# Second block of a one-core kernel: where the convolution's gate and norm, the last head steps, the key and query norms and the first expert products stand

## The chip, the cores and the metric

The kernel runs on one core of a Trainium2 chip. The metric is the device time of one execution in microseconds. The core has five engines that run their own instruction lists: PE (matrix products), ACT and DVE (element by element), POOL, and SP, which here issues nearly all loads. Engines wait for each other through semaphores.

## The reference

256 tokens of width 1024 pass two blocks. The first (a pooling mixer, an attention, two MLPs) is not touched. The second is, cut to what matters:

```python
hn = rms_norm_2(h, attn_norm_g)
xc, b_gate, c_gate, q, k, v = split(hn @ w_in)
y = b_gate * causal_depthwise_conv(c_gate * xc, conv_w)      # width 512, 3 taps
y_conv = rms_norm_2(y in groups of 64) * conv_out_g
q = rms_norm_2(q, per 64) * q_norm_g / 8 ; k = rms_norm_2(k, per 64) * k_norm_g
a = softmax(q0 k0^T) - lam * softmax(q1 k1^T)                # 4 heads of 128, causal
y_attn = rms_norm_2(a @ v, per head) * subln_g * (1 - lam_init)
h = h + concat(y_conv, y_attn) @ w_out
hn2 = rms_norm_2(h)
g = argmax(hn2 @ w_router_group)                             # 1 of 4 groups
top 2 of the 8 experts of that group, softmax of the two
h = h + sum over 32 experts: comb * ((silu(hn2 @ w_gate) * (hn2 @ w_up)) @ w_down)
```

## The kernel before

**Weights.** All weights are fp32 in DRAM. Class Weights streams them in order through a ring of 1 MB slots: `pump` issues a load on SP (L90) whenever the slot that was used longest ago is free. A dense weight is used in halves of 128x1024: `split` writes a high part on ACT (L107) and the rest on DVE (L108), the tile wp; when the second half of a slot is split, the slot is free. `take()` hands out the next half, `look(n)` splits n halves ahead, `W.ahead` is the number that `take` splits ahead by itself, `W.held` keeps slots from being used again. `open_ring`, `state_ring` and `parts_ring` turn memory that has become free into further slots. The 32 experts' weights are used whole, with no split; `W.done(NE)` frees four slots after half of a gate, up or down product. An expert's capacity is a tile of CAP tokens, and four experts (NE) make one pass p; eight passes (NP) do all 32.

**Order.** Every engine runs its instructions in the order in which the Python code issues them; nothing reorders them afterwards. Generators (`proj`, `proj_tok`, `normed`, `conv_out`) are advanced by `steps`, so that the code writes by hand which piece of a product or a norm comes next. PSUM has four single banks (tag A) and two pairs (tag B).

**Key and query norms.** `proj` makes q (pq) and k (pk), `proj_tok` makes v (pv). `normed` has three steps: squares (gq), then the mean by a product (gstat) with c2 added (kn, L909) and Ln and Exp on ACT (L911, L912), then `newton` (ku, L300 to L304) and the scaling that gives kn (L917). `x_tokens` turns the residual into tokens (product xkb, copy xk L1034); `x_stat_end` gives the mean of squares xstat, from which `rsq` makes r (ry on ACT L310 and L311, ru and r on DVE), and c2 is made from it (L1072). rt and tcol bring r and c2 into columns. The queries' sums of squares are the 16 small products qs, then qa and rq. The tiles gq, kn, ku, ry and ru share six buffers of the tag t2, taken in turn.

**Heads.** `h0(h)` makes the scores z, the maxima m (L934) and the softmax pr (ACT L940, DVE L944 to L948); `h1` transposes it (L955), `h2` multiplies with v and squares, `h3` takes the mean and Ln and Exp, `h4` ends the norm with `newton` and splits the result into mh and ml (L317, L318), the input of the last product wout.

**Convolution.** pc, px, pb are the three projections; `conv_u` and `conv_y` (yc, L995) make the taps, `conv_gate` multiplies by b_gate and squares, `conv_out(i)` takes the mean by a product, adds c2 (cn, L1015), Ln, Exp, `newton` and two splits into mh and ml. `out_piece(s)` is a quarter of half of the product with w_out; pieces 0 to 3 use the heads, 4 to 7 the convolution.

**Experts.** `h_add` adds the residual (xk), `h_transpose` and `logits` lead to the router on DVE; warm products keep PE at work; rank (five products), rk (L1310), the one-hot oh, `gather` (32 records of gb, then eight copies xg), `first_products` (gu), `hidden`, `down_products` (dn).

```python
    nk = normed(steps(pk, 4), kn, g2[:, 1:2])
    steps(nk)
    steps(pq, 2)
    x_tokens(0, 0)
    steps(pq)
    x_tokens(0, 1)
    p = x_stat_end(xs, "A")
    rsq(p, EPS, r, T)
    DVE.tensor_scalar(c2, p, EPS, EPS, op0=OP.add, op1=OP.mult)
```

## Time and profile before

| | |
|---|---|
| median of 3 runs | 1117.42 us (1117.38 to 1337.03) |
| profiled execution: its own time, its span | 1116.21 us, 1114.5 us |
| mean granted clock of PE | 0.969 of full |
| PE busy | 981.5 us, 88% of the span |
| DVE busy | 485.4 us, 44% |
| ACT busy | 389.6 us, 35% |
| loads | 306.58 MB, mean 275 GB/s over the span |

Busy shares are averages over stages with different limits. All times below are us from the start of the span of the profiled execution. [...] A matmul in the rows may count as two records where it makes two passes.

### The profile page before, as it was taken

What the parts mean: (1) busy time and instruction counts of PE and PEld (TensorE: products, weight loads), DVE (VectorE), ACT (ScalarE), POOL (GpSimd) and SP (SyncE); (2) the same over time, 40 slices, a digit from 0 to 9 for tenths busy, and PEclk for the clock granted to TensorE, in tenths of its full rate; (3) what the DMA queues carried; (4) which work ended last, traced back from release to release, by engine and by line L of the source; (5) the groups of instructions that cost most, each with busy time, mean ns of one, the idle gap of its engine ahead of it and who ended that gap; (6) DMA issues with size and microseconds to landing.
All of it is one profiled execution on the core that took longest, in us unless ns stands there. A gap on an engine that the chain in (4) does not pass through costs nothing.

```text
span 1114.5 us, 16629 instructions
## 1 busy us (share of the span) xinstructions
PE 981.5 (88%) x6999; PEld 729.9 (65%) x6999; DVE 485.4 (44%) x843; ACT 389.6 (35%) x602; POOL 11.4 (1%) x31
## 2 busy tenths in 40 slices
PE   9899999999999999999999989887777766777666
PEld 7899999998889999999979764232222221212212
DVE  8865554795448845655987763010101010100101
ACT  6554444563766534444566522000000000000000
POOL 3000000000000000000000000000000000000000
PEclk9999999999999999999999999999989999888997
DMA  8465565437222654555374787999999999999997
GB/s 310 146 226 186 199 195 188 151 115 256 84 77 81 242 200 159 168 211 189 107 309 152 264 330 313 421 420 421 420 422 421 420 422 421 421 421 420 421 412 260
DMA packets 79895, 306.58 MB, mean 275 GB/s; under 512 B 8033, under 2 KB 13770, under 8 KB 56266
## 3 DMA queue, kind: packets, MB, share of 16 engines
q1 hardware_dynamic: 79818, 305.49, 71.4%
q8 instruction: 56, 0.92, 0.3%
q14 instruction: 21, 0.17, 0.0%
HBM read 304.42 MB, written 1.05 MB: 274 GB/s over the span
## 4 chain that ended last, share of the span: by engine, by line
PE 51%; DMA 37%; DVE 8%; ACT 3%; issue 1%; SPq 0%; DVEq 0%; ACTq 0%
PE pj L156 20%; PE acc L156 17%; DMA w<-in_w_exp_up 12%; DMA w<-in_w_exp_gate 12%; DMA w<-in_w_exp_down 12%; PE z L156 3%; PE wo L156 2%; PE pv L156 2%; PE gu L156 1%; DVE xT L450 1%; DVE wp L108 1%; DVE xt L447 1%; PE wout L156 1%; DVE xl L453 1%; ACT wp L107 1%
## 5 line engine op out<-in xcount | busy, mean ns | idle before, releaser
L108 DVE TENSOR_TENSOR wp<-w,wp 128x1024 fp32r<-128x1024 f32 x194 | 230.4, 1223 | 86.1 <-ACT wp L107 86.0
L156 PE MATMUL gu<-w,xg 128*32 128x512 f32 x1024 | 186.7, 654 | 75.0 <-DMA w<-in_w_exp_up 43.6
L107 ACT ACTIVATE wp<-w 128x1024 fp32r<-128x1024 f32 x194 | 196.3, 1050 | 87.2 <-PE pj L156 41.8
L156 PE MATMUL acc<-uh,wp 128*128 128x256 f32 x1024 | 187.0, 283 | 0.0
L156 PEld LDWEIGHTS gu<-w,xg 128*32 128x32 f32 x1024 | 40.6, 118 | 206.0 <-DMA w<-in_w_exp_up 77.0
L156 PE MATMUL pj<-xh,wp 128*128 128x256 f32 x1216 | 173.0, 284 | 1.9 <-DVE ev L406 1.9
L156 PEld LDWEIGHTS acc<-uh,wp 128*128 128x128 f32 x1024 | 160.7, 192 | 0.1
L156 PEld LDWEIGHTS pj<-xh,wp 128*128 128x128 f32 x1216 | 157.2, 192 | 2.7 <-PE px L156 2.4
L156 PE MATMUL acc<-ul,wp 128*128 128x256 f32 x512 | 144.9, 283 | 0.0
L156 PE MATMUL dn<-w,sT 128*32 128x512 f32 (+1 forms) x544 | 82.1, 627 | 33.6 <-DMA w<-in_w_exp_down 23.9
L156 PE MATMUL pj<-xl,wp 128*128 128x256 f32 x608 | 98.4, 283 | 0.0
L156 PEld LDWEIGHTS acc<-ul,wp 128*128 128x128 f32 x512 | 98.3, 192 | 0.1
L156 PEld LDWEIGHTS pj<-xl,wp 128*128 128x128 f32 x608 | 84.1, 192 | 0.0
L318 DVE TENSOR_TENSOR yl<-dn,yh 128x512 fp32r<-128x512 f32 x15 | 10.4, 692 | 164.5 <-ACT yh L317 164.5
L156 PEld LDWEIGHTS dn<-w,sT 128*32 128x32 f32 x544 | 21.2, 118 | 88.0 <-DMA w<-in_w_exp_down 43.4
L317 ACT ACTIVATE yh<-dn 128x512 fp32r<-128x512 f32 x15 | 9.0, 597 | 197.0 <-PE dn L156 128.7
L1409 DVE SCALAR_TENSOR_TENSOR silu<-silu,cs,gu 128x512 f32<-128x512 f32 x8 | 8.9, 1108 | 133.3 <-PE gu L156 133.3
L1336 ACT ACTIVATE xg<-gb,ffn 128x128 f32<-128x128 f32 x32 | 9.2, 369 | 128.7 <-PE gb L156 128.7
L532 DVE TENSOR_TENSOR usq<-relu 128x512 f32<-128x512 f32 x32 | 22.0, 687 | 48.9 <-ACT relu L531 48.9
L156 PE MATMUL px<-xh,wp 128*128 128x256 f32 x224 | 33.2, 291 | 4.4 <-ACT wp L107 3.4
L531 ACT ACTIVATE relu<-pj 128x512 f32<-128x512 f32 x28 | 16.4, 587 | 56.4 <-PE pj L156 56.4
L156 PEld LDWEIGHTS gb<-oh,xk 128*128 128x128 f32 x256 | 29.2, 192 | 7.4 <-PE gu L156 4.2
(353 smaller groups left out, 1038.9 us busy)
## 6 DMA issues: line engine op xcount, KB each, us to landing
w<-in_w_exp_gate SPq DMA_DIRECT2D x64, 1024.0 KB, 19.9
w<-in_w_exp_up SPq DMA_DIRECT2D x64, 1024.0 KB, 19.8
w<-in_w_exp_down SPq DMA_DIRECT2D x60, 1024.0 KB, 19.8
w<-in_w_down SPq DMA_DIRECT2D x32, 1024.0 KB, 5.8
w<-in_w_up SPq DMA_DIRECT2D x28, 1024.0 KB, 7.1
w<-in_w_in SPq DMA_DIRECT2D x10, 1024.0 KB, 12.2
w<-in_w_kv SPq DMA_DIRECT2D x6, 1024.0 KB
w<-in_w_up SPq DMA_DIRECT2D x8, 512.0 KB
```

The lines of the kernel that those rows point to most:

```text
L107: self.nc.scalar.activation(h, raw, AF.Copy)
L108: self.nc.vector.tensor_tensor(lo, raw, h.bitcast(F32), OP.subtract)
L156: PE.matmul(o, l, r, start=start, stop=stop, skip_group_check=True)
L317: ACT.activation(h, src, AF.Copy)
L318: DVE.tensor_tensor(lo, src, h.bitcast(F32), OP.subtract)
L447: DVE.scalar_tensor_tensor(t, self.y[:, k] if k < 2 else self.banks[k // 2][:, (k % 2) * 256:(k % 2 + 1) * 256], self.gain(k), self.r, op0 ...
L450: DVE.tensor_tensor(xT[:, k], xT[:, k], t, OP.add)
L453: DVE.scalar_tensor_tensor(lo[l], xT[:, l], g(l), h[l].bitcast(F32), op0=OP.mult, op1=OP.subtract)
L531: ACT.activation(r, b[i], AF.Relu)
L532: DVE.tensor_tensor(u, r, r, OP.mult)
L1336: ACT.activation(dst, src, AF.Identity, scale=g)
L1409: DVE.scalar_tensor_tensor(sv, sv, CSL[p][1], of(u), op0=OP.mult, op1=OP.mult)
```

## The change

In the first part (before the first head) xstat, c2 and the Ln and Exp of r are issued ahead of the first `x_tokens`, the key norm's second step comes after the third step of pq, r's Newton step after it; the key norm's last step moves behind rt and tcol, and the qs products are issued in four groups of two between the matmuls of the first step of pv (`query_stat`); `W.look(5)` goes. In the second part (after `conv_y(1)`) the last projection pb yields after each of its four half pieces; `h4(2)`, `h3(3)`, `conv_gate`, `h4(3)` and the first step of `conv_out(0)` stand between them, `W.ahead` is set to 2 and then 0, single `look(3)` calls take the place of the `look(6)` calls, and the closing of the attention's memory, with the ring slots that it gives, comes after the whole of pb. In the third part the two warm matmuls behind rank write a bank of their own; `gather` stops after 12 of its 16 gb products and the first half of the first gate product comes ahead of the last four; xg is written by ACT and DVE in turn.

```diff
--- before.py
+++ after.py
@@ -476,7 +476,7 @@
         return p
-    def proj(xh, xl, tag="B", stagger=None, turned=False, post=None):
+    def proj(xh, xl, tag="B", stagger=False, turned=False, post=None):
         b = [post.px[:, i] for i in range(2)] if post else pair(tag, "pj")
@@ -500,10 +500,8 @@
             two = [W.take(), W.take()]
             for i in range(2):
                 for s in (2, 3):
-                    if s == 3:
-                        stagger(None, i)
                     piece(s, *two[s - 2], (2 * i, 2 * i + 1))
-                stagger(b[i], i)
+                    yield b
         if post:
             b = post.whole()
             W.ahead = was
@@ -696,7 +694,7 @@
                        channel_multiplier=-1)
     V = st.tile([128, 2, D], F32, name="V", tag="xtok")
-    def proj_tok(xh, xl, tag):
+    def proj_tok(xh, xl, tag, between=iter(())):
         b = pair(tag, "pv")
         for s in range(4):
@@ -708,6 +706,7 @@
                     for t in range(2):
                         mm(b[t], a[k][:, t * 128:(t + 1) * 128], w[:, c], start=k == 0 and w is h and a is xh,
                            stop=k == 7 and a is xl)
+                    next(between, None)
             yield None
         yield b
@@ -995,18 +994,9 @@
                 DVE.scalar_tensor_tensor(yc[:, k], src, w, yc[:, k], op0=OP.mult, op1=OP.add)
     def conv_gate(b, i):
-        if b is None:
-            if i == 0:
-                h3(3)
-                h4(2)
-                h4(3)
-        else:
-            v = flat(yc[:, 2 * i:2 * i + 2])
-            DVE.tensor_tensor(v, v, b, OP.mult)
-            cq.append(norm_square(v, 512))
-            if i == 0:
-                aq_stack.close()
-                open_ring("ring0", RINGS[1])
+        v = flat(yc[:, 2 * i:2 * i + 2])
+        DVE.tensor_tensor(v, v, b, OP.mult)
+        cq.append(norm_square(v, 512))
     def conv_out(i):
         b = bb[i]
@@ -1034,9 +1024,19 @@
         ACT.activation(dst, of(b), AF.Copy)
     pq, pk = proj(anh, anl, "B", turned=True), proj(anh, anl, post=P)
-    pv = proj_tok(anh, anl, "A")
+    def query_stat():
+        for t in range(2):
+            for j in range(4):
+                o = t * 8 + 2 * j
+                mm(qs[:, o:o + 2], sq[j // 2][:, (j % 2) * 256 + t * 128:(j % 2) * 256 + (t + 1) * 128], blk2, start=True,
+                   stop=True)
+                if j % 2:
+                    yield
+    pv = proj_tok(anh, anl, "A", query_stat())
     cq = []
-    pc, px, pb = proj(anh, anl, "A"), proj(anh, anl, "A"), proj(anh, anl, "A", conv_gate)
+    pc, px, pb = proj(anh, anl, "A"), proj(anh, anl, "A"), proj(anh, anl, "A", True)
     def steps(g, n=1):
         for _ in range(n):
@@ -1064,12 +1064,16 @@
     nk = normed(steps(pk, 4), kn, g2[:, 1:2])
     steps(nk)
     steps(pq, 2)
+    p = x_stat_end(xs, "A")
+    DVE.tensor_scalar(c2, p, EPS, EPS, op0=OP.add, op1=OP.mult)
+    y, ry = [tmp.tile([128, 512], F32, name="ry", tag="t2", bufs=6)[:, :T] for _ in range(2)]
+    ACT.activation(y, p, AF.Ln, bias=eps)
+    ACT.activation(y, y, AF.Exp, scale=-0.5)
     x_tokens(0, 0)
     steps(pq)
+    steps(nk)
+    newton([(p, EPS, y, ry, r)])
     x_tokens(0, 1)
-    p = x_stat_end(xs, "A")
-    rsq(p, EPS, r, T)
-    DVE.tensor_scalar(c2, p, EPS, EPS, op0=OP.add, op1=OP.mult)
     u = act.tile([128, 4 * (T + 2)], F32, name="u", tag="x3").rearrange("p (k t) -> p k t", t=T + 2)
     POOL.memset(u[:, :, 0:2], 0.0)
     steps(pq)
@@ -1078,7 +1082,6 @@
     x_tokens(1, 0)
     x_tokens(1, 1)
     state_ring("xT")
-    steps(nk)
     rt = bank("A", "rt")
     for i, a in enumerate((r, c2)):
@@ -1089,17 +1092,12 @@
     DVE.scalar_tensor_tensor(r, r, 0.25, r, op0=OP.mult, op1=OP.mult)
     rcol = aq.tile([128, 2], F32, name="rcol")
     DVE.tensor_scalar(rcol, tcol[:, 0:2], -0.5, None, op0=OP.mult)
+    steps(nk)
     qs = bank("A", "qs")
-    for t in range(2):
-        for j in range(4):
-            o = t * 8 + 2 * j
-            mm(qs[:, o:o + 2], sq[j // 2][:, (j % 2) * 256 + t * 128:(j % 2) * 256 + (t + 1) * 128], blk2, start=True,
-               stop=True)
+    steps(pv)
     qa = aq.tile([128, 2, 8], F32, name="qa")
     for t in range(2):
         DVE.tensor_scalar(qa[:, t], qs[:, t * 8:(t + 1) * 8], tcol[:, 2 + t:3 + t], None, op0=OP.add)
-    steps(nk)
     new_mix(mixh, 1, "mh", "uh")
     new_mix(mixl, 1, "ml", "ul")
     for i in range(2):
@@ -1107,8 +1105,7 @@
     rsq(flat(qa), 0.0, flat(rq), 16)
     DVE.tensor_scalar(rq, rq, -0.5, None, op0=OP.mult)
     gate_consts()
-    W.look(5)
-    steps(pv, 2)
+    steps(pv)
     h0(0)
     steps(pv)
     vb = steps(pv, 2)
@@ -1144,14 +1141,28 @@
     h1(3)
     h3(2)
     conv_y(1)
+    h4(2)
     steps(pb)
     h2(3)
     conv_y(2)
     new_mix(mixl, 0, "ml", "x3")
+    W.ahead = 2
+    steps(pb)
+    h3(3)
     bb = steps(pb)
+    conv_gate(bb[0], 0)
+    steps(pb)
+    h4(3)
+    co = [conv_out(0), conv_out(1)]
+    steps(co[0])
+    W.ahead = 0
+    W.look(3)
+    steps(pb)
+    conv_gate(bb[1], 1)
+    aq_stack.close()
+    open_ring("ring0", RINGS[1])
     state_ring("xh")
     state_ring("xl")
-    W.look(6)
     ob = [two_banks("wout") for _ in range(2)]
@@ -1164,17 +1175,18 @@
                     mm(ob[t][:, i], a[k][:, f], w[:, i * 512:(i + 1) * 512], start=s == 0 and w is h and a is mixh,
                        stop=s == 7 and a is mixl)
-    co = [conv_out(0), conv_out(1)]
     out_piece(0, *W.take())
     steps(co[0])
+    steps(co[1])
+    W.look(3)
     out_piece(1, *W.take())
+    W.look(3)
     steps(co[1])
+    out_piece(2, *W.take())
+    W.look(3)
     W.held = True
-    W.look(6)
-    steps(co[0])
-    out_piece(2, *W.take())
+    W.look(5)
     parts_ring()
-    steps(co[1])
     out_piece(3, *W.take())
     parts_ring()
@@ -1305,7 +1317,7 @@
             mm(o, onesb, sel[:, 0], stop=True)
     for t in range(2):
         mm(rkp[:, 64:96], onesb, sel[:, t], stop=t == 1)
-    warm(rkp[:, 128:384], xk[:, 0, 0:T], 2, ident)
+    warm(bank("A", "warm")[:, :T], xk[:, 0, 0:T], 2, ident)
     rk = small("rk", 2, 32)
     DVE.scalar_tensor_tensor(rk, rkp[:, 0:64].rearrange("p (t e) -> p t e", t=2), 1.0, sel, op0=OP.add, op1=OP.mult)
@@ -1321,22 +1333,41 @@
     def gather(p):
         XG[p] = hx.tile([128, KT, 128], F32, name="xg", tag="hx")
         for i in range(2):
             b = bank("A", "gb")
             for j in range(4):
+                if i and j == 2:
+                    yield
                 f = slice((4 * i + j) * 128, (4 * i + j + 1) * 128)
                 for t in range(2):
                     mm(b[:, j * 128:(j + 1) * 128], xk[:, t, f], OHT[p][t], start=t == 0 and j == 0, stop=t == 1)
             for j in range(4):
                 dst, src, g = XG[p][:, 4 * i + j], b[:, j * 128:(j + 1) * 128], ffn[:, 4 * i + j:4 * i + j + 1]
-                if i:
+                if j % 2:
                     DVE.tensor_scalar(dst, src, g, None, op0=OP.mult)
                 else:
                     ACT.activation(dst, src, AF.Identity, scale=g)
+        yield
+    def first_products(p, i, halves_=range(2), b=None):
+        b = bank("A", "gu") if b is None else b
+        for h in halves_:
+            n = 6 * NE * p + 2 * NE * i + NE * h
+            for kk in range(4):
+                k = 4 * h + kk
+                for j in range(NE):
+                    mm(b[j * CAP:(j + 1) * CAP], XG[p][:, k, j * CAP:(j + 1) * CAP],
+                       W.whole(n + j)[:, kk * 512:(kk + 1) * 512], start=k == 0, stop=k == 7)
+            W.done(NE)
+        return b
     onehot(0)
-    gather(0)
+    first_gather = gather(0)
+    next(first_gather)
+    first_gate = first_products(0, 0, (0,))
+    next(first_gather)
     ms, rr, u = sm[:, 0:2], sm[:, 4:6], sm[:, 6:8]
     DVE.tensor_tensor(ms, sm[:, 0:4:2], sm[:, 1:4:2], OP.add)
     DVE.tensor_scalar(ms, ms, 1.0 / D, EPS, op0=OP.mult, op1=OP.add)
@@ -1389,18 +1420,6 @@
                                  accum_out=c[:, NE + 1:NE + 2])
         DVE.tensor_copy(c[:, NE:NE + 1], b[:, 256 + NE:257 + NE])
         CSL[p] = ot, c[:, NE + 1:NE + 2], c[:, NE:NE + 1]
-    def first_products(p, i, halves_=range(2), b=None):
...
     def hidden(p, g, u):
         s = mo.tile([128, 512], F32, name="silu", tag="silu")
@@ -1452,7 +1471,7 @@
     for p in range(NP):
         if p:
             y = parts_of(YS[p - 1][0])
-        g = first_products(p, 0, (0,))
+        g = first_products(p, 0, (0,)) if p else first_gate
         if p:
             combine(p - 1, y, 0, 512)
             y = parts_of(YS[p - 1][1])
@@ -1465,7 +1484,8 @@
         u = first_products(p, 1)
         s = hidden(p, g, u)
         if p + 1 < NP:
-            gather(p + 1)
+            for _ in gather(p + 1):
+                pass
         sT = down_products(p, s)
         if p == 1:
```

How the lists of three engines change, with the waits as the compiled program has them.

ACT, from the wp copy after the squares of the keys; before (xk is the residual in tokens, ry and kn are Ln and Exp of r and of the key norm, gq squares):

```order
L107 ACTIVATE wp<-w 128x1024 [waits PE_49]
L1034 ACTIVATE xk<-xkb 128x128x4 [waits PE_49]
L107 ACTIVATE wp<-w 128x1024 [waits DMAHW1_49]
L1034 ACTIVATE xk<-xkb 128x128x4 [waits PE_49]
L310 ACTIVATE ry<-xstat,eps 128x256 [waits PE_49]
L311 ACTIVATE ry<-ry 128x256 [waits Activation_49]
L107 ACTIVATE wp<-w 128x1024
L895 ACTIVATE gq<-pj 128x512 [waits PE_49]
L895 ACTIVATE gq<-pj 128x512
L1034 ACTIVATE xk<-xkb 128x128x4 [waits PE_49] x2
L911 ACTIVATE kn<-kn 128x512 [waits DVE_49,Activation_49]
L912 ACTIVATE kn<-kn 128x512 [waits Activation_49]
```

and after:

```order
L107 ACTIVATE wp<-w 128x1024 [waits PE_49]
L1070 ACTIVATE ry<-xstat,eps 128x256 [waits DVE_49]
L1071 ACTIVATE ry<-ry 128x256 [waits Activation_49]
L1024 ACTIVATE xk<-xkb 128x128x4 [waits PE_49]
L107 ACTIVATE wp<-w 128x1024 [waits DMAHW1_49]
L910 ACTIVATE kn<-kn 128x512 [waits DVE_49]
L911 ACTIVATE kn<-kn 128x512 [waits Activation_49]
L910 ACTIVATE kn<-kn 128x512 [waits DVE_49]
L911 ACTIVATE kn<-kn 128x512 [waits Activation_49]
L1024 ACTIVATE xk<-xkb 128x128x4 [waits PE_49]
L107 ACTIVATE wp<-w 128x1024
L894 ACTIVATE gq<-pj 128x512 [waits DVE_49,PE_49]
```

The Ln of xstat (L310, now L1070) has moved ahead of the first xk copy and waits for DVE where it waited for PE; the keys' Ln and Exp (L911, now L910) now stand ahead of the last three xk copies, of a wp copy and of the queries' squares.

DVE at the same place; before (c_5881 is c2, ku the Newton step of the key norm):

```order
L1072 TENSOR_SCALAR c_5881<-xstat 128x256
L108 TENSOR_TENSOR wp<-w,wp 128x1024 [waits PE_49,Activation_49]
L909 TENSOR_TENSOR kn<-gstat,c_5881 128x512 [waits DVE_49,PE_49]
L909 TENSOR_TENSOR kn<-gstat,c_5881 128x512 [waits PE_49]
L1088 COPY tcol<-rt 128x4 [waits PE_49]
L1089 SCALAR_TENSOR_TENSOR r<-r 128x256
L1091 TENSOR_SCALAR rcol<-tcol 128x2 [waits DVE_49]
L1101 TENSOR_SCALAR qa<-qs,tcol 128x8 [waits PE_49]
L1101 TENSOR_SCALAR qa<-qs,tcol 128x8
L300 TENSOR_TENSOR ku<-kn 128x512 [waits Activation_49]
```

and after:

```order
L1068 TENSOR_SCALAR c_5881<-xstat 128x256 [waits PE_49]
L108 TENSOR_TENSOR wp<-w,wp 128x1024 [waits DMAHW1_49,Activation_49]
L908 TENSOR_TENSOR kn<-gstat,c_5881 128x512 [waits DVE_49,PE_49]
L908 TENSOR_TENSOR kn<-gstat,c_5881 128x512 [waits PE_49]
L300 TENSOR_TENSOR ry<-ry 128x256
L302 SCALAR_TENSOR_TENSOR ry<-xstat,ry 128x256 [waits DVE_49]
L304 SCALAR_TENSOR_TENSOR r<-ry 128x256 [waits DVE_49]
L108 TENSOR_TENSOR wp<-w,wp 128x1024 [waits Activation_49]
L1091 COPY tcol<-rt 128x4 [waits PE_49]
L1092 SCALAR_TENSOR_TENSOR r<-r 128x256 [waits DVE_49]
L1094 TENSOR_SCALAR rcol<-tcol 128x2 [waits DVE_49]
L300 TENSOR_TENSOR ku<-kn 128x512 [waits PE_49,Activation_49]
```

c2 has moved between wp subtractions, r's Newton step behind the key norm's kn; qa no longer stands ahead of ku, and the first ku waits for PE too (the third group of qs, which reads the buffer that ku takes).

PE at the end of the second block, from the last rank product; before:

```order
L156 MATMUL rank<-bf 128x32
L156 MATMUL rank<-xk,ident 128x256 x2
L156 MATMUL gb<-oh,xk 128x128 [waits DVE_49,PE_49]
L156 MATMUL gb<-oh,xk 128x128 [waits DVE_49]
L156 MATMUL gb<-oh,xk 128x128 x6
L156 MATMUL gb<-oh,xk 128x128 [waits PE_49]
L156 MATMUL gb<-oh,xk 128x128 x7
L156 MATMUL gu<-w,xg 32x512 [waits DMAHW4_49,Activation_49]
L156 MATMUL gu<-w,xg 32x512 [waits DMAHW5_49]
L156 MATMUL gu<-w,xg 32x512 [waits DMAHW6_49]
L156 MATMUL gu<-w,xg 32x512 [waits DMAHW7_49]
L156 MATMUL gu<-w,xg 32x512 [waits Activation_49]
```

and after:

```order
L156 MATMUL rank<-bf 128x32
L156 MATMUL warm<-xk,ident 128x256 [waits PE_49]
L156 MATMUL warm<-xk,ident 128x256
L156 MATMUL gb<-oh,xk 128x128 [waits DVE_49,PE_49]
L156 MATMUL gb<-oh,xk 128x128 [waits DVE_49]
L156 MATMUL gb<-oh,xk 128x128 x6
L156 MATMUL gb<-oh,xk 128x128 [waits PE_49]
L156 MATMUL gb<-oh,xk 128x128 x3
L156 MATMUL gu<-w,xg 32x512 [waits DMAHW4_49,Activation_49]
L156 MATMUL gu<-w,xg 32x512 [waits DMAHW5_49]
L156 MATMUL gu<-w,xg 32x512 [waits DMAHW6_49]
L156 MATMUL gu<-w,xg 32x512 [waits DMAHW7_49]
```

The two small matmuls write warm where they wrote rank, and the first half of the gate product (gu) stands between 12 gb products and the last four.

SP in the middle of the convolution, loads of the first experts' up weights (a piece of the difference):

```order
-L90 DMA w<-in_w_exp_up 128x2048 [waits DMAHW4_49,DVE_49]
-L90 DMA w<-in_w_exp_up 128x2048 [waits DMAHW5_49,PE_49,Pool_49]
-L90 DMA w<-in_w_exp_up 128x2048 [waits DMAHW6_49,PE_49]
-L90 DMA w<-in_w_exp_up 128x2048 [waits DMAHW7_49,PE_49]
+L90 DMA w<-in_w_exp_up 128x2048 [waits DMAHW4_49,PE_49,Pool_49]
+L90 DMA w<-in_w_exp_up 128x2048 [waits DMAHW5_49,PE_49]
+L90 DMA w<-in_w_exp_up 128x2048 [waits DMAHW6_49,PE_49]
+L90 DMA w<-in_w_exp_up 128x2048 [waits DMAHW7_49,DVE_49]
 L90 DMA w<-in_w_exp_up 128x2048 [waits DMAHW0_49,DVE_49]
```

The first load of this piece that waits for a split on DVE was the first; now it is the fourth.

## Rows read from the trace of the kernel before

**Rows 1.** Chain of waits, two of its DMA pieces (start us, us, what).

```profile
685.06 18.22 DMA w<-in_w_exp_gate
...
1063.47 19.51 DMA w<-in_w_exp_up
```

**Rows 2.** Timeline of SP (start us, us of issuing, queue, line, load).

```profile
650.27 0.33 SPq L90 DMA_DIRECT2D w<-in_w_exp_up  x1
...
677.34 0.33 SPq L90 DMA_DIRECT2D w<-in_w_exp_down  x1
```

**Rows 3.** Stretches of 2 us: busy time by engine, granted clock, DMA share, GB/s.

```profile
646.00:648.00 2.00, 2.00 (x5) 1.61 (x6) 1.51 (x4) 0.42 (x1) 0.00 (x0) 0.50 0.35 147
...
672.00:674.00 2.00, 2.00 (x20) 1.73 (x23) 0.13 (x1) 1.15 (x4) 0.00 (x0) 1.00 0.09 29
...
678.00:680.00 2.00, 2.00 (x24) 0.65 (x20) 1.31 (x9) 0.61 (x1) 0.00 (x0) 1.00 0.89 201
```

**Rows 4.** Costliest groups on the page (count | busy, mean ns | idle before, releaser).

```profile
L108 DVE TENSOR_TENSOR wp<-w,wp 128x1024 fp32r<-128x1024 f32 x194 | 230.4, 1223 | 86.1 <-ACT wp L107 86.0
...
L107 ACT ACTIVATE wp<-w 128x1024 fp32r<-128x1024 f32 x194 | 196.3, 1050 | 87.2 <-PE pj L156 41.8
```

**Rows 5.** Timeline of DVE, key norm (last bracket: idle before, releaser).

```profile
564.01 1.28 DVE L909 TENSOR_TENSOR kn<-gstat,c 128x512 f32<-128x512 f32 x2
565.21 0.15 DVE L1088 COPY tcol<-rt 128x4 f32<-128x4 f32 x1
...
567.44 0.68 DVE L300 TENSOR_TENSOR ku<-kn 128x512 f32<-128x512 f32 x1
...
572.45 0.75 DVE L917 SCALAR_TENSOR_TENSOR kn<-ev,g,ku 128x512 f32<-128x512 f32 x1
...
576.63 0.42 DVE L934 TENSOR_REDUCE m<-z 128x2 f32<-128x256 f32 x1
```

**Rows 6.** Timeline of ACT, same stretch.

```profile
560.36 0.44 ACT L310 ACTIVATE ry<-xstat,eps 128x256 f32<-128x256 f32 x1
...
563.06 2.00 ACT L1034 ACTIVATE xk<-xkb 128x512 f32<-128x512 f32 x2
564.84 0.65 ACT L911 ACTIVATE kn<-kn 128x512 f32<-128x512 f32 x1
```

**Rows 7.** Timeline of PE, query sums to the second head.

```profile
565.12 2.01 PE L156 MATMUL qs<-blk,gq 128*128 128x2 f32 x16 [0.25 <-ACT xk L1034]
566.98 2.06 PE L156 MATMUL pv<-wp,xh 128*128 128x512 f32 x4
...
582.04 0.44 PE L955 MATMUL z<-ident,pr 128*128 128x128 f32 x2 [0.39 <-DVE pr L948]
```

**Rows 8.** Timelines of DVE and PE, convolution and last product.

```profile
625.49 0.42 DVE L300 TENSOR_TENSOR h<-h 128x256 f32<-128x256 f32 x1
...
645.87 2.07 PE L156 MATMUL wout<-wp,mh 128*128 128x512 f32 x4 [3.28 <-ACT mh L317]
...
648.60 1.18 PE L156 MATMUL wout<-wp,mh 128*128 128x512 f32 x4
...
651.44 1.07 PE L156 MATMUL wout<-wp,mh 128*128 128x512 f32 x4
...
652.80 1.07 PE L156 MATMUL wout<-wp,mh 128*128 128x512 f32 x4
...
658.27 0.62 PE L156 MATMUL wout<-wp,ml 128*128 128x512 f32 x2
```

**Rows 9.** Timelines of PE and DVE, from rank to the first gate product.

```profile
668.03 1.11 PE L156 MATMUL rank<-xk,ident 128*128 128x256 f32 x4
...
669.18 0.23 DVE L1310 SCALAR_TENSOR_TENSOR rk<-rank,bf 128x64 f32<-128x64 f32 x1 [1.42 <-PE rank L156]
...
669.95 3.81 PE L156 MATMUL gb<-oh,xk 128*128 128x128 f32 x32 [0.81 <-DVE oh L1318]
673.69 7.08 PE L156 MATMUL gu<-w,xg 128*32 128x512 f32 x64
```

More of the change, by code (lines that the diff above doesn't have):

```diff
@@ L1391, in slot_side @@
         CSL[p] = ot, c[:, NE + 1:NE + 2], c[:, NE:NE + 1]
-    def first_products(p, i, halves_=range(2), b=None):
-        b = bank("A", "gu") if b is None else b
-        for h in halves_:
-            n = 6 * NE * p + 2 * NE * i + NE * h
-            for kk in range(4):
-                k = 4 * h + kk
-                for j in range(NE):
-                    mm(b[j * CAP:(j + 1) * CAP], XG[p][:, k, j * CAP:(j + 1) * CAP],
-                       W.whole(n + j)[:, kk * 512:(kk + 1) * 512], start=k == 0, stop=k == 7)
-            W.done(NE)
-        return b
     def hidden(p, g, u):
```

## The prediction

> **What bounds the kernel now.** I read the chain of waits first. From 685.06 on it consists of DMA pieces of one kind, some twenty of about 19.8 us, with the last long one ending at 1063.47 + 19.51 [rows 1]: the last 430 us are a stream of expert weights that never stops, and PE's 88% busy share says nothing about them. So this change, all of it ahead of 690 us, can move the end only through the moment at which that stream starts, and each us there is a us at the end. The windows of 2 us show the moment: the queues carry almost nothing from 672 and run again from 678 [rows 3]. The SP timeline tells what they waited for: the load issued at 677.34 is the first that needs a slot freed by the first half of the first gate product gu [rows 2, 9]. Ahead of that, eight loads issued from 650.27 on had kept the queues busy until 671.8. So two things decide: when PE reaches the end of the first half of gu (here called T, 677.3), and when the loads issued before it are through (671.8, so 5.5 us of slack). Up to 589 us and from there to T, PE's own timeline says how a delay passes: from the second head's scores to the convolution's end PE has no idle time on it, so what comes late there stays late.
>
> **First part, the norms.** I walk the new lists with durations of before; a wp part is 1.05 on ACT and 1.22 on DVE [rows 4].
> - c2 now stands on DVE behind three wp subtractions and is done at 559.85, where the Ln of xstat, which reads the same bank, now waits for it. Before it started at 560.36 without such a wait [rows 6]; now 559.9. Ln and Exp (0.44 and 0.42) and one xk copy and one wp follow to 562.65, so DVE's wp and the adds kn (1.28 for two, before at 564.01 [rows 5]) run to 565.2: no change so far.
> - Now the keys' Ln and Exp go first on ACT: 564.5 to 567.1 (four of about 0.65, from 564.84 before [rows 6]). Behind them queue an xk copy (1.0 each, 2.00 for two [rows 6]) to 568.1, a wp to 569.0, two gq squares (before 1.06 for both, at 562.11) to 570.1, another xk copy to 571.05. PE waits for exactly these: it has xkb, then rt, then pv and the interleaved qs behind them. So qs, at 565.12 before [rows 7], starts at 571.05. tcol on DVE moves from 565.21 [rows 5] to 570.35 in the same way, behind r's Newton step and a wp.
> - The first ku takes the buffer that the first squares of the queries had, so it waits for the third of the four qs groups. That is three groups of four records of 0.117 (2.01 for 16, overlapped [rows 7]) and two pv pairs between them of 0.45 (2.06 for four at half clock, 1.07 at full): 571.05 + 1.41 + 0.9 = 573.4. Before it started at 567.44, and from there to the end of kn took 5.76 us (572.45 + 0.75) [rows 5]. So kn ends at 579.2.
> - Behind kn on DVE stand a wp (1.2), qa (0.36), Ln and Exp on ACT (0.5), rq (0.8), the memsets (0.45) and a wp (1.2): the first maximum m, at 576.63 before [rows 5], starts at 583.6. The softmax behind it is the same 5.4 us, and the second head's scores, which wait for it on PE (582.04 [rows 7]), come at 589.1. **+7.0 us**. Before, m had come late for PE by only 0.4 us of idle time there [rows 7], so all of this shows.
>
> The waits leave PE idle twice, from 567.1 to 571.1 and from 584.6 to 588.4. [...] Both new idle times are longer than 3.28, so I take a fall behind each and 1.37 us for it: the first falls on the qs groups that ku waits for, the second on products with no slack. **+2.7 us.** The bound below is nothing, above about 2 us each, since the second head's products are short.
>
> [...]
>
> Up to 620 nothing else moves and PE is without idle time, so +9.8 arrives there whole.
>
> **Second part, the convolution.** In before's time, DVE's list after conv_y(1) (619.8) now reads: h4(2) (four steps of 0.42 to 0.48 [rows 8], split behind it), a wp to 624.35, last taps 625.9, gate 626.5, h4(3) and split 629.25, c2 added 629.85, ACT's Ln and Exp, a wp to 633.4, second gate 634.0, Newton and two splits 638.8, second norm's add 639.4, Ln, Exp, two wp to 644.1, Newton and two splits 648.9, then three wp to 650.65, 651.8 and 652.9. PE waits twice in the projection (about 1.9 and 2.4 us, at 621.5 and 632.3) and then for the wp at 650.65 ahead of the last four steps of 1.36 with a few transposes, and ends the product at 658.8. Before it ended at 658.27 + 0.62 [rows 8], with the 3.28 us of idle time and the slow step in it. So the moved steps fill the old gap and open new ones: **0 for PE**. That rests on a chain of 30 us of DVE and ACT, and its bounds are wide: if it ran no longer than PE's own work there, PE would save the 6.0 us of idle time that it has from 626 to 646 and the slow step's 1.4, 7.4 together; if each of its dozen hand-overs between ACT and DVE costs 0.3 more than I took, it is 4 us later.
>
> Loads: SP is in order. The fourth and fifth up load now wait for splits on DVE, the fifth for the one at 650.65, and behind it stand seven more that before went partly earlier. From then on eleven loads have to pass where before eight did after 650.27 [rows 2]. At 2.49 us for a load (19.8 us in flight, eight at a time [rows 1]) they are through at 678.8, at the 2.7 us each that the eight took at 680.3.
>
> **Third part, the experts.** rk was issued when rank's bank was free, after the warm products (668.03 + 1.11; rk at 669.18 [rows 9]). With warm in a bank of its own rk comes 0.9 us sooner, gb 0.75. The first half of gu starts after 24 of 32 gb records of 0.119 (3.81 for 32 [rows 9]), 0.9 sooner. So T is 1.6 us earlier, 675.7 in before's time. But the loads are through only at 678.8, and stream and T are not added: the later one counts. Before it was T with the stream at 678.2; now it is the loads: **+0.6 us**, and the 1.6 are worth nothing. ACT and DVE now take turns on one bank of gb; each xg is 0.3 to 0.4 us and a quarter of the half product is 0.88, so that hides.
>
> **Sum.** 1116.21 (the profiled execution's own time) + 7.0 + 2.7 + 0 + 0.6 = 1126.5; the median of the runs shown is 1.2 higher, so **1127.8**, 0.9% slower. A difference under 2%, 22 us, is about what a measurement of this kernel can't tell from none.
>
> **Rivals.**
> - The clock does not fall behind the new idle times. For it: behind the qs products of before PE ran slower too, with almost no idle time, so idle time is not the only cause. Against it: the row at 646. 1127.8 − 2.7 = 1125.1. Chance 0.15.
> - [...] Chance 0.15.
> - *Not slower.* The convolution's chain is short enough to be hidden by PE's products: the wp that I put at 650.65 comes by 643, PE never waits for it, the loads behind it go early too, and T counts again. Then 1127.8 − 7.4 − 0.6 − 1.6 = 1118.2, no difference. It decides between the two at 7.4 us less on that chain of 30; from there on each us less is nothing. For it: half of the steps only trade places with wp subtractions, and the list says order, not time. Against: every row has its duration. Chance 0.12.
> - The chain is longer, 4 us, which delays the wp, the loads and the end: 1131.8. Chance 0.1.
> - The walk holds: 0.48, from 1126 to 1130.
>
> The range 1117 to 1132 takes in all but the tails of the third and fourth. Over 2% either way would need 22 us: faster 0.01, slower 0.02, within 0.97.
>
> **What would show it in the changed kernel's profile.** qs begins some 6 us later than before, the first ku right after a qs group, m about 7 us later, PE idle for some 4 us ahead of it and a granted clock of 0.5 behind. In the convolution, a wait of PE for a wp ahead of wout's second half, and no idle queue between the eleven loads and the expert stream. Wrong would be: qs at 565 to 567, or PE with no idle time from 620 to 646, or queues idle until T.

## The result, and the profile after

The changed kernel takes 1125.15 us (median of 5 runs, 1124.22 to 1125.61) against 1117.42 before: 1.0067 times the time, 95% interval 1.0054 to 1.0080. One execution of before took 1337.03 us, a slow one, and stands in no ratio. The profiled execution took 1125.15 us with a span of 1123.4, 8.9 more than before's 1114.5. The forecast was 1127.8, 0.9% slower, in a range of 1117 to 1132. The interval leaves out 1, so 0.7% can be told from nothing here, which the prediction doubted.

The norms, timeline of DVE of the changed kernel:

```profile
559.55 0.42 DVE L1068 TENSOR_SCALAR c<-xstat 128x256 f32<-128x256 f32 x1
...
563.89 1.28 DVE L908 TENSOR_TENSOR kn<-gstat,c 128x512 f32<-128x512 f32 x2
...
574.73 0.69 DVE L300 TENSOR_TENSOR ku<-kn 128x512 f32<-128x512 f32 x1 [4.13 <-PE qs L156]
...
584.89 0.42 DVE L933 TENSOR_REDUCE m<-z 128x2 f32<-128x256 f32 x1
```

ACT in the same stretch:

```profile
560.01 0.47 ACT L1070 ACTIVATE ry<-xstat,eps 128x256 f32<-128x256 f32 x1 [2.10 <-DVE c L1068]
...
564.61 0.63 ACT L910 ACTIVATE kn<-kn 128x512 f32<-128x512 f32 x1 [1.89 <-DVE kn L908]
```

PE, from the value product's first matmuls to the second head's scores:

```profile
568.06 0.49 PE L156 MATMUL pv<-wp,xh 128*128 128x512 f32 x1 [0.93 <-ACT xk L1024]
570.25 0.50 PE L156 MATMUL pv<-wp,xh 128*128 128x512 f32 x1 [1.69 <-DVE tcol L1091]
570.85 0.61 PE L156 MATMUL qs<-blk,gq 128*128 128x2 f32 x4
...
589.61 0.30 PE L954 MATMUL z<-ident,pr 128*128 128x128 f32 x1 [1.78 <-DVE pr L947]
590.30 0.44 PE L954 MATMUL z<-ident,pr 128*128 128x128 f32 x2 [0.39 <-DVE pr L947]
590.67 0.93 PE L156 MATMUL z<-kn,qn 64*128 64x128 f32 x8
```

These stand against [rows 5 to 7]. The Ln of xstat has waited 2.10 us for c2; the adds kn start where they did (563.89, before 564.01); qs starts 5.7 later, ku waits 4.13 for the query products and starts 7.3 later, m 8.3 later, and so do the transposes of the first head (590.30, before 582.04). Windows of 2 us (busy time by engine, granted clock, DMA share, GB/s):

```profile
572.00:574.00 2.00, 2.00 (x9) 1.73 (x8) 0.00 (x0) 1.69 (x3) 0.00 (x0) 0.50 0.97 387
...
588.00:590.00 2.00, 0.30 (x1) 0.14 (x1) 1.54 (x6) 2.00 (x4) 0.00 (x0) 1.00 0.54 225
...
644.00:646.00 2.00, 2.00 (x5) 1.34 (x4) 1.48 (x4) 0.42 (x1) 0.00 (x0) 0.50 0.23 94
...
678.00:680.00 2.00, 2.00 (x21) 2.00 (x20) 0.10 (x1) 0.37 (x1) 0.00 (x0) 1.00 1.06 442
...
684.00:686.00 2.00, 1.54 (x16) 1.05 (x20) 0.35 (x1) 0.54 (x2) 0.00 (x0) 1.00 0.99 397
```

The clock is at 0.50 (in the windows from 572 to 578) while qs and pv run, and at 1.00 behind the wait ahead of the second head. The queues are full at 678 and at 684: the gap of before (DMA share 0.09 in the window at 672 [rows 3]) is gone.

The last product and the gate product, PE:

```profile
642.87 1.71 PE L156 MATMUL pj<-gq,blk 128*128 128x512 f32 x2 [2.12 <-ACT gq L894]
643.59 2.70 PE L156 MATMUL wout<-wp,mh 128*128 128x512 f32 x4
...
658.82 0.73 PE L156 MATMUL wout<-wp,mh 128*128 128x512 f32 x2 [0.55 <-DVE wp L108]
...
666.71 0.62 PE L156 MATMUL wout<-wp,ml 128*128 128x512 f32 x2
...
677.43 2.92 PE L156 MATMUL gb<-oh,xk 128*128 128x128 f32 x24
680.28 3.64 PE L156 MATMUL gu<-w,xg 128*32 128x512 f32 x32
```

and SP, the fifth up load and the first load that waits for the gate product:

```profile
658.79 0.33 SPq L90 DMA_DIRECT2D w<-in_w_exp_up  x1
...
683.93 0.33 SPq L90 DMA_DIRECT2D w<-in_w_exp_down  x1
```

The product with w_out ends 8.44 later than before (666.71 against 658.27 [rows 8]), the gate product's first half is through 6.6 later (T: 683.93 against 677.34 [rows 2]), and the whole 8.9 later. The third part has gained 1.85 on T, and the end has not got it.

### The profile page after: what moved, and what is told of

Same layout as the page of the kernel before. It is cut to its first block, busy times and chain, and to the rows that moved or that the text cites. A ratio compares the mean times of both kernels' runs of the same rounds, so it can differ in the third digit from the quotient of the medians.

```text
span 1123.4 us, 16630 instructions
## 1 busy us (share of the span) xinstructions
PE 987.9 (88%) x6999; PEld 730.6 (65%) x6999; DVE 488.0 (43%) x843; ACT 392.5 (35%) x602; POOL 11.3 (1%) x31
## 3 DMA queue, kind: packets, MB, share of 16 engines
HBM read 304.42 MB, written 1.05 MB: 272 GB/s over the span
## 4 chain that ended last, share of the span: by engine, by line
PE 48%; DMA 37%; DVE 10%; ACT 3%; issue 2%; SPq 0%; ACTq 0%; DVEq 0%
PE pj L156 19%; PE acc L156 17%; DMA w<-in_w_exp_up 12%; DMA w<-in_w_exp_gate 12%; DMA w<-in_w_exp_down 12%; PE z L156 3%; PE pv L156 2%; PE wo L156 2%; DVE wp L108 2%; DVE xT L450 1%; DVE xt L447 1%; PE gu L156 1%; DVE xl L453 1%; ACT wp L107 1%; PE wout L156 1%
## 5 line engine op out<-in xcount | busy, mean ns | idle before, releaser
L156 PE MATMUL gu<-w,xg 128*32 128x512 f32 x1024 | 190.4, 675 | 69.5 <-DMA w<-in_w_exp_up 38.9
L1351 ACT ACTIVATE xg<-gb,ffn 128x128 f32<-128x128 f32 x32 | 11.8, 368 | 137.8 <-PE gb L156 131.1
```

Source lines behind the costliest of these rows:

```text
L156: PE.matmul(o, l, r, start=start, stop=stop, skip_group_check=True)
L1351: ACT.activation(dst, src, AF.Identity, scale=g)
```

## The experiments

Ratios are to the kernel before on the same chip, with 95% intervals; its median was 1117.2, 1116.2 and 1117.0 us in the three groups of four. Each kernel ran 5 or 11 times (pv_warm 4 times); a profile shows one of these executions, not always the middle one. Theory N: the later key norm, passed on whole by PE, is the loss; the convolution's steps are neutral on PE but hold back the loads; these decide the end, so that the third part's gain is not used. Rival C: the moved convolution steps are the loss.

**The first part taken back (norms_undone).**

```diff
-    pv = proj_tok(anh, anl, "A", query_stat())
+    pv = proj_tok(anh, anl, "A")
...
     x_tokens(0, 1)
+    p = x_stat_end(xs, "A")
+    rsq(p, EPS, r, T)
+    DVE.tensor_scalar(c2, p, EPS, EPS, op0=OP.add, op1=OP.mult)
...
     state_ring("xT")
+    steps(nk)
...
+    W.look(5)
+    steps(pv, 2)
```

> The first part of the change (key and query norms) is taken back, the second and third stay. If the norms carry the loss and the convolution only puts the loads behind one split, as the prediction has it: 1118.0, 0.6 us above before, with the queues busy without a gap from about 650.7 on and the first half of the first gate product some 2 us earlier than before without use. If the convolution's moved steps carry the loss: 1124 to 1125. If the loads do not decide and the earlier gate product counts: 1115.7.

Measured: 1117.43 us, 0.9997 (0.9988 to 1.0006). The loss is gone: rival C falls. The time is a little under the 1118.0 expected and above the 1115.7 of a gate product that decides. T was at 675.73, 1.6 sooner than before, and not used. Windows of this kernel ahead of T:

```profile
672.00:674.00 2.00, 2.00 (x22) 0.68 (x24) 0.40 (x2) 0.37 (x1) 0.00 (x0) 1.00 1.03 430
674.00:676.00 2.00, 2.00 (x20) 0.61 (x12) 0.00 (x0) 0.00 (x0) 0.00 (x0) 1.00 1.01 418
```

**Only the first part (norms_only).** The first part's hunks of the diff put into the kernel before, nothing else.

> Only the first part of the change. If the norms carry the loss: the second head's scores 8.3 us later than before and all of it at the end, 1125.7, as much as the whole change or a little more. If the convolution carries it: 1117.4 to 1119.

Measured: 1125.01 us, 1.0066 (1.0052 to 1.0080), the whole change's loss. In its profile (1126.97, the slowest of its five executions) T is 11.3 later, not 8.3: the clock was at 0.50 for longer (653 to 660) and fell once more at 674.

**The convolution as before (conv_undone).** The first and third part's hunks, not the second's.

> The first and third part, the convolution as before. By the prediction's steps the loads are then through in time, the gate product decides, and its 1.7 us count: 1117.4 + 8.3 - 1.7 = 1124.0. If the third part is worth nothing anywhere: 1125.7. If the convolution carries the loss: 1117.

Measured: 1123.08 us, 1.0047 (1.0034 to 1.0061), 2 us less than norms_only, all five runs of the one under all five of the other. Without the second part the third part's gain counts.

**Only the third part (experts_only).**

```diff
-    warm(rkp[:, 128:384], xk[:, 0, 0:T], 2, ident)
+    warm(bank("A", "warm")[:, :T], xk[:, 0, 0:T], 2, ident)
...
-    gather(0)
+    first_gather = gather(0)
+    next(first_gather)
+    first_gate = first_products(0, 0, (0,))
+    next(first_gather)
```

> Only the third part. If the first half of the gate product decides when the stream of loads starts, it comes 1.6 to 1.85 us sooner and so does the end: 1115.7. If the loads before it decide, or the earlier start is lost to DVE and ACT taking turns on the gb bank: 1117.4.

Measured: 1115.63 us, 0.9984 (0.9975 to 0.9993): 1.8 us faster than before by the ratio. T decides here; the queues are empty ahead of it:

```profile
672.00:674.00 2.00, 2.00 (x23) 0.68 (x25) 0.53 (x2) 0.37 (x1) 0.00 (x0) 1.00 0.19 70
674.00:676.00 2.00, 2.00 (x22) 0.56 (x15) 0.00 (x0) 0.00 (x0) 0.00 (x0) 1.00 0.00 0
```

**The experts as before (experts_undone).** The third part's hunks taken out of the changed kernel.

> The first and second part, the experts as before. In the changed kernel the queues run without a gap from the fifth up load on, so the gate product's 1.85 us are not used: by that the same time as the changed kernel, 1125.2 (at most 0.3 more). If the third part counts there too: 1127.0.

Measured: 1125.14 us (1.0084, 1.0068 to 1.0099). In microseconds that is the changed kernel's 1125.15; the ratios (1.0084 against 1.0067, each to its own runs of before) overlap, but their middles are 1.9 us apart, as the other reading has it. The profiles tell the two apart: T is at 685.90, 2 us later, the fifth up load at 658.90 against 658.79, and the span is 1123.2 against 1123.4.

**The loads freed earlier (loads_early).** norms_undone with one edit; the wp subtraction that frees the fifth up load's slot moves ahead of the second conv norm's Newton step.

```diff
     out_piece(1, *W.take())
-    W.look(3)
+    W.look(4)
     steps(co[1])
```

> The kernel without the first part (norms undone), with one more half of the output weights split ahead of the second conv norm's Newton step, so that the fifth up load is free some 5.7 us sooner. If the loads queued behind that split took the 1.7 us that the earlier gate product gives: they are through in time now, the queues stand idle again ahead of the gate product's release, and the time is that of the third part alone, 1115.5. If the third part's gain went elsewhere: 1117.4 as before this edit.

Measured: 1114.30 us, 0.9976 (0.9966 to 0.9986), against 0.9997 without the edit: 2.4 us, more than the 1.9 expected, and with experts_warm (1114.51) the lowest time here. The fifth up load goes at 646.52 where it went at 650.61 (4.1 sooner, 5.7 expected), with T all but unmoved at 675.52. Its queues do not stand empty, as I had expected. They are full up to 674 and only run down around T, where those of norms_undone are at 1.01 and 1.04:

```profile
674.00:676.00 2.00, 2.00 (x21) 0.82 (x14) 0.00 (x0) 0.00 (x0) 0.00 (x0) 1.00 0.94 385
676.00:678.00 2.00, 1.54 (x18) 0.75 (x20) 0.53 (x2) 0.73 (x2) 0.00 (x0) 1.00 0.87 242
```

Two sums over the profiles show which side decides:

| kernel | T | span − T | fifth up load | span − that |
|---|---|---|---|---|
| before | 677.34 | 437.2 | earlier | |
| experts_only | 675.86 | 437.1 | earlier | |
| norms_only | 688.66 | 436.6 | earlier | |
| conv_undone | 684.42 | 437.0 | earlier | |
| changed kernel | 683.93 | 439.5 | 658.79 | 464.6 |
| norms_undone | 675.73 | 440.0 | 650.61 | 465.1 |
| experts_undone | 685.90 | 437.3 | 658.90 | 464.3 |
| loads_early | 675.52 | 438.2 | 646.52 | 467.2 |

With the convolution as before the end is T + 437. With the change it is the fifth up load + 464 to 465, and T is then 2.5 to 3 too early to matter; in experts_undone both hold. The kernels below fit too: span − T is 437.0 in ln_first and 436.7 in ln_ku and experts_warm, span − load 465.0 in ku_own and pv_warm and 464.5 in two_warm. The row of loads_early fits neither sum: T + 437 would be 1112.5 and the span was 1113.7. Its profiled execution is 1.1 over its median, and its first down load, which waits for a later split, goes 1.3 later than in norms_undone (654.22 against 652.88); which of the two it is stays open. So the gain of 2.4 shows that the split ahead of the fifth up load is what held the end, and not that T alone decides once it is moved.

**The Newton step in kn's own tile (ku_own).** The wait of ku for qs goes, since another buffer is written.

```diff
-            u = tmp.tile([128, 512], F32, name="ku", tag="t2", bufs=6)
+            u = flat(dst[:, 2 * i:2 * i + 2])
```

> The changed kernel with the key norm's Newton step working in kn's own tile, so that it does not wait for the query products that read the buffer. If that wait is the largest part of the norms' loss: the first ku at about 570.6 where it is 574.7, the second head's scores about 4 us earlier, and 1121.2 at the end. If PE, late by the copies of the tokens, is what makes the heads late anyway: 1125.2.

Measured: 1123.27 us, 1.0061 (1.0047 to 1.0074); experts_undone, which is as slow as the changed kernel, took 1125.14 on the same chip. So a gain of about 2, half of the expected; by the ratios alone (1.0061 against 1.0067 of the changed kernel) it would not be clear. DVE and PE:

```profile
570.69 0.68 DVE L300 TENSOR_TENSOR kn<-kn 128x512 f32<-128x512 f32 x1
...
583.98 0.42 DVE L933 TENSOR_REDUCE m<-z 128x2 f32<-128x256 f32 x1 [3.04 <-PE z L156]
```

```profile
578.88 1.91 PE L156 MATMUL pv<-wp,xh 128*128 128x512 f32 x4
...
582.69 0.93 PE L156 MATMUL z<-kn,qn 64*128 64x128 f32 x8
...
589.77 0.93 PE L156 MATMUL z<-kn,qn 64*128 64x128 f32 x8
```

The Newton step starts 4.0 sooner, as expected, but then m waits 3.04 for the first head's scores z: PE, with qs and pv late and at a clock of 0.50 (in the windows from 572 to 580), has become the limit. The second head's scores come 0.9 sooner, not 4.

**c2 behind the Ln (ln_first).**

```diff
-    DVE.tensor_scalar(c2, p, EPS, EPS, op0=OP.add, op1=OP.mult)
     y, ry = [tmp.tile([128, 512], F32, name="ry", tag="t2", bufs=6)[:, :T] for _ in range(2)]
     ACT.activation(y, p, AF.Ln, bias=eps)
     ACT.activation(y, y, AF.Exp, scale=-0.5)
+    DVE.tensor_scalar(c2, p, EPS, EPS, op0=OP.add, op1=OP.mult)
```

> The changed kernel with c2 issued behind the Ln and Exp of xstat, so that the Ln does not wait for DVE's turn on the bank. If the turn costs what the walk gives, the copy of the tokens and everything behind it on ACT come 2 us earlier and the end is at 1123.1. If the wait is hidden (ACT idle later anyway): 1125.2.

Measured: 1121.44 us, 1.0051 (1.0038 to 1.0065), 3.7 less than experts_undone on the same chip (1.8 less than the changed kernel if the ratios 1.0051 and 1.0067 are compared; 2.1 was expected). All five runs are under all five of experts_undone. The adds kn start at 561.58 (2.3 sooner), the second head's scores at 587.50 (3.2 sooner: of the four groups of query products two take 0.85 us at the lower clock, in the changed kernel three).

**Both (ln_ku).**

> The changed kernel with both edits of the norms: c2 behind the Ln and Exp of xstat, and the Newton step in kn's own tile. Alone they gave 3.7 and 1.9 us. If the wait for the bank's turn and the wait for the query products stand one behind the other on one chain, 1119.6; if PE, late by the copies of the tokens, bounds the second head's scores once the first is gone, 1121 to 1121.4.

Measured: 1121.78 us, 1.0045 (1.0031 to 1.0059): not below ln_first alone by anything that these intervals show. In its profile m waits 1.62 for z, so PE is the limit there, as the second reading expected. But the second head's scores come at 586.08, 1.4 sooner than in ln_first, and that execution (1119.39) is the fastest of the five, 2.4 under the median. So the gains do not add in full, and whether a part of the second comes through is open.

**Products without use in the first wait (pv_warm).**

```diff
         b = pair(tag, "pv")
+        if hasattr(between, "gi_frame"):
+            warm(b[0][:, 0:128], ident, 8, ident)
```

> The changed kernel with eight small products without use (their result is overwritten) ahead of the value product, in the time in which PE waits. If the clock falls there because PE stood idle, it stays at 1.00 from 571.5 to 577.5, the query products end about 1.4 us sooner and the end is at 1123.8. If the clock falls all the same, as it did behind the query products of the kernel before: 1125.2.

Measured: 1126.66 us, 1.0095 (1.0080 to 1.0110), from four runs: no gain, though the clock did what was hoped for. Windows and PE:

```profile
572.00:574.00 2.00, 2.00 (x16) 1.83 (x16) 0.71 (x2) 1.55 (x3) 0.00 (x0) 1.00 0.99 408
...
590.00:592.00 2.00, 2.00 (x15) 1.35 (x12) 1.36 (x2) 0.22 (x1) 0.00 (x0) 0.50 0.00 0
```

```profile
571.73 0.51 PE L156 MATMUL qs<-blk,gq 128*128 128x2 f32 x4
572.10 0.71 PE L156 MATMUL pv<-wp,xl 128*128 128x512 f32 x2
572.65 0.50 PE L156 MATMUL qs<-blk,gq 128*128 128x2 f32 x4
...
588.12 0.30 PE L956 MATMUL z<-ident,pr 128*128 128x128 f32 x1 [3.60 <-DVE pr L949]
...
589.43 1.65 PE L156 MATMUL z<-kn,qn 64*128 64x128 f32 x8
```

At a clock of 1.00 a group of qs takes 0.50 and a pair of pv 0.71, where they took 0.85 and 1.20 at 0.50 in the changed kernel; ku starts at 573.25 (1.5 sooner). But PE then has nothing left, waits 3.60 instead of 1.78, and the clock falls behind that wait: the scores take 1.65 where they took 0.93. One fall was traded for the other.

**Products without use in both waits (two_warm).** Fourteen more, ahead of the first head's transposes:

```diff
+    warm(qs[:, 128:256], ident, 14, ident)
     h1(0)
     h0(1)
```

> The changed kernel with products without use in both idle times of the first part: ahead of the value product, and in the 4.2 us ahead of the first head's transposes. With the first alone the clock stayed up in the value product and fell behind the second idle time instead. If one fall was only traded for the other, both together give the 1.4 us: 1123.8. If not: 1125.2 or more.

Measured: 1122.83 us, 1.0054 (1.0040 to 1.0068). Against pv_warm's 1.0095 that is clear; against the changed kernel's 1.0067 the intervals overlap, so the 1.4 us are borne out in size but not shown by the time alone. In the profile the clock stays at 1.00 through this stretch (every window from 556 to 656) and the second head's scores come at 589.17, 1.5 sooner than in the changed kernel.

**Products without use ahead of the convolution's split (experts_warm).**

```diff
     out_piece(3, *W.take())
+    warm(bank("A", "warm"), xk[:, 0, 0:512], 3, ident)
```

> The third part alone, with three products without use in a free bank in the 3.3 us in which PE waits for the convolution's first split at 642.4 to 645.9. If the fall of the granted clock behind that idle time costs the 1.37 us worked out from the rows of before, the first gate product is that much earlier and the end at 1114.3. If the clock falls at another place for it, or the stream then waits for its loads: 1115.6.

Measured: 1114.51 us, 0.9977 (0.9968 to 0.9986), against 0.9984 without: the intervals overlap, inconclusive. In its profile the clock falls at 582 and 664 (0.54 and 0.52 in those windows), in that of experts_only at 568 and 646 (0.50 and 0.55). The fall at 646 is gone and one at 664 has come; that at 582 stands ahead of the edit, so the edit did not move it there.

## Why the prediction was right, and where its size was off

**The norms: right, step by step.** c2 at 559.55 (walked: its end at 559.85), the Ln at 560.01 (559.9), the adds ending at 565.17 (565.2), qs at 570.85 (571.05), and with the first fall of the clock added, ku at 574.73 (573.4 + 1.4), m at 584.89 (583.6 + 1.4), the second head's scores at 590.67 where they had been at 582.40: +8.27 (7.0 + 1.4). norms_only shows that this alone is the loss, ln_first and ku_own show two links of the chain. Both together (ln_ku) give back 2.5 to 3.4 of the 7.7; the rest, the keys' Ln and Exp ahead of the copies on ACT and the dropped `W.look(5)`, was traced or left as it is, and not undone by itself. That ku's wait for a buffer costs what it lasts was wrong as a reading: without it PE is the next to be late by almost as much.

**The first fall: right in size, on another ground.** I took it from one idle time of 4 us, longer than the 3.28 of before, behind which the window at 646 is at 0.50 and one step of the last product took 2.73 us (645.87 to 648.60) where a step takes 1.36 (651.44 to 652.80) [rows 3, 8]; the difference is the 1.37 that was counted for a fall. PE waited 0.93 and 1.69 instead, with one short product between (568.06, 570.25), both far under 3.28, and the clock fell all the same. Before had a fall there too (0.72 in the window at 566, 0.50 at 568), behind the qs products and with 0.25 us of idle time ahead of them (pv takes 2.06 for four [rows 7]). That the waits have to do with it is borne out by pv_warm and two_warm: with products in them the clock stayed at 1.00 in both, while it fell to 0.50 there in all seven other profiles with the moved first part. It is one profile each, and with the first part as before the fall is missing in two of five profiles without any edit there, so it is not more than borne out.

**The second fall: wrong, and it is the term that was mis-sized.** I counted a fall behind each of two idle times, 2.7 together. The first made pv slow (1.20 us for two, 0.71 in pv_warm), so PE had work until 587.8, the second idle time was 1.78 instead of 3.8, and the clock was 1.00 behind it. In pv_warm, where the first does not come, the second does. The two terms of a sum excluded each other; this is the 1.4 by which the profiled execution's 8.9 falls short of the forecast 10.3.

The same exchange stands in kernels whose instructions up to there are those of before. PE of experts_only:

```profile
581.45 0.30 PE L955 MATMUL z<-ident,pr 128*128 128x128 f32 x1 [0.34 <-DVE pr L948]
...
582.51 0.93 PE L156 MATMUL z<-kn,qn 64*128 64x128 f32 x8
```

and of experts_warm:

```profile
581.32 0.30 PE L955 MATMUL z<-ident,pr 128*128 128x128 f32 x1 [1.93 <-DVE pr L948]
...
582.55 1.66 PE L156 MATMUL z<-kn,qn 64*128 64x128 f32 x8
```

In experts_only the clock falls at 568 (0.50 in that window), pv is slow (four at 569.26 take 1.91 us) and PE waits 0.34 for the softmax, with no fall behind (1.00 at 582). In experts_warm it does not fall at 568 (1.00; four of pv at 569.81 take 1.07), pv is done sooner, PE waits 1.93 and the clock falls at 582 (0.54). Over all 14 profiles, ten have the first fall alone, three the second alone (pv_warm, loads_early, experts_warm), two_warm has none, and none has both.

**Passed through: right.** +8.27 at the second head, +8.28 at the last head's value product (627.66 against 619.38), +8.44 at the end of the product with w_out. The ground given for it (no idle time of PE up to the convolution's end) is a misreading: before has 6.0 us of it between 626 and 646, as the prediction's second part itself counts. There the work of DVE and ACT that PE waits for came late by as much.

**The convolution: right in sum, partly by chance.** 0 was forecast, 0.16 measured. The split that PE and the load wait for ended just ahead of the load at 658.79, 650.5 in before's time, where the walk had 650.65. The wait of 2.12 ahead of 642.87 was in the walk (2.4), the fall of the clock at 643 to 647 behind it (0.50 in the window at 644) was not, and before's fall at 646 went.

**The loads: right.** They begin at the fifth up load and do not stop after 662 (DMA share 1.01 to 1.05 in every 10 us up to 1112); the end came 0.6 later than the 8.3 account for, as forecast. One step of that 0.6 is not written out: 650.65 + 11 x 2.49 is 678.0, not 678.8, so by the terms shown the loads would not have come later than before at all. loads_early takes the second part's hold on the loads away, and there the second part does no harm that the intervals show.

**The third part: right.** 1.85 sooner (1.6 forecast), not used in the changed kernel, used in experts_only and conv_undone.

**qs between the products of pv:** no row shows the query products to cost less there than alone. At a clock of 1.00 (pv_warm) a qs group and a pv pair together take 0.92 us (571.73 to 572.65), the 0.47 and 0.45 of each alone (in before 1.86 for 16 of qs, 565.12 to 566.98, and 1.36 for six of pv, 571.34 to 572.70).

**The number: nearer to a rival's than to its own, by chance.** The forecast is 2.65 over the measured 1125.15. 1.4 of it is the second fall; 1.2 is the distance of before's profiled execution from its median, which was added on and which the changed kernel's profiled execution does not have (single executions of before lie between 1115.4 and 1119.9 on the three chips). 0.1 is a slip: 7.0 + 2.7 is 9.7, not 9.8. So the time lies below the 1126 to 1130 of the walk and on the 1125.1 of the first rival, whose condition held only in half: the clock did fall behind the first of the new waits.

## What to carry to other kernels

Where a long stream of loads ends the kernel, find every event at which that stream can start, and add the time behind each; the change's worth is read from the latest, and an earlier product is worth nothing while one blocked load holds back those that the same engine issues behind it (here six more went out within 3.2 us of the fifth up load). Before moving a norm, walk all engines' lists at once: what passes ahead of a short copy on ACT delays PE, and PE then delays the very norm (here qs came 5.7 us later and ku waited 4.13 us for it). Two costs that come from the same idle engine are not to be added before asking whether the first removes the second.

## What was not expected of the hardware

The granted clock fell to 0.50 behind a wait of 2.12 us with one short product behind it (642.87) and behind waits of 0.93 and 1.69 (570.25), while a wait of 1.78 us (589.61) left it at 1.00. So the length of the last wait did not tell by itself whether it falls. And the same list of instructions, with the same waits ahead of it, stayed at 0.50 for different times: from 571 to 578 in the changed kernel, to 582 in experts_undone, whose instructions up to there are the same; the first head's scores started at 581.07 in one and 582.61 in the other. With the first part as before the fall came at 567 to 568 in three profiles and at 582 to 583 in two. Differences of 1 to 2 us between single profiles of these kernels are of that kind.
